# The norm's input transposed by the host: scaling x^T in place, with only the inverse roots turned on TensorE

## The chip, the cores and the metric

The kernel runs on one core of a Trainium2 chip. The metric is the device time of one execution in microseconds. The core has TensorE (PE in the profile, its weight loads PEld), VectorE (DVE), ScalarE (ACT), GpSimd (POOL) and SyncE (SP), which here does nothing but start DMA transfers, all in one queue. Each engine takes its own instructions strictly in the order in which the program holds them, and waits on semaphores for what other engines and transfers deliver.

## The reference

One block of a streaming encoder over 2048 tokens of width 1024, in float32. What matters here is its beginning:

```
xn = rms_norm(h, norm_gain[layer])          # x * rsqrt(mean(x*x) + eps) * gain
proj = xn @ w_in[layer]
qa, ka, va, ga, qb, kb, vb, gb, iq, ik, iw, za, zb = jnp.split(proj, offsets, axis=-1)
```

Two kinds of attention follow, one over neighbouring chunks, one over the 256 keys per query that an indexer (`iq`, `ik`, `iw`) picks; then gates, an output product and a second norm. A product on TensorE contracts over the partitions of both operands, so `xn` is needed with the 1024 features on partitions (8 slices of 128) and the tokens along the free axis: as x^T.

## The kernel before

Tokens are taken in 16 tiles of 128, in the order `order = [8..15, 0..7]`. A first stage goes over the tiles once: it norms a tile, keeps it transposed and split into a rounded high part `xh` and the rest `xl` (three products of such parts replace one in full precision), and projects it on 424 columns (`wih`, `wil`) for the indexer and the shared key and value of the second attention. `xh` and `xl` have two slots of 512 tokens each; for the first eight tiles both are also written to DRAM (`xsD`) and read back much later. Then the main stage multiplies `xh`, `xl` with all other columns of the weights (`acc` in the rows), while the indexer's logits and the search for the top keys run beside it; attention and output follow.

The functions of the first stage, in the order of the code: `load_x` starts a tile's transfer two tiles ahead; `norm` squares the tile on ScalarE with a sum (`sq`, `ss`), takes ten small VectorE steps to the inverse root (`rsqrt`, L141 to L147), scales the tile in place by root and gain (L248), turns it on TensorE in 8 pieces of 128x128 (L253, into PSUM tiles `tr` and `trl`), and splits it (L256 on ScalarE, L257 on VectorE, both from PSUM). `project` has 24 matmuls of 424 columns (L274), then a copy `tok` on ScalarE (L278) and 13 small GpSimd steps for the rotary angles (`rope`, and L281). `keys` splits key and indexer key (`kk`), turns three pieces (L304) and stores them. `prep` fetches and splits the weights of the main stage (L172 to L176: a copy that gates the transfer, ScalarE's rounding, GpSimd's subtraction). The loop calls `norm(i + 1)`, `project(i)`, `keys(i - 1)`.

The code's order isn't the program's: a scheduler takes what is ready by its own estimate and fixes the order of each engine before the run, so matmuls of the main stage can stand among those of the last projections, and the pieces of `norm` for one tile among steps of others. Buffers come from pools; a tile with the same tag waits until the one before it is free.

## Time and profile before

| what | value |
|---|---|
| time, median of 3 runs | 2105.91 us (2104.52 to 2106.01) |
| time of the profiled execution | 2103.23 us |
| its span | 2101.3 us |
| TensorE busy | 2033.5 us, 97% |
| VectorE, ScalarE, GpSimd busy | 65%, 58%, 42% |
| granted TensorE clock, mean | 0.997 |

The median lies 2.7 us above the profiled execution, whose time has 1.9 us outside its span. "Busy" counts overlapping instructions once. The page's 40 slices are 52.5 us each; the first stage is the first two and a bit.

### The profile page before, as it was taken

To read this page: it belongs to the slowest core of one execution; us is meant where nothing else is said; L and a number is where in the kernel's file an instruction comes from. 1 tells how busy PE (TensorE), PEld (TensorE's weight loads), DVE (VectorE), ACT (ScalarE), POOL (GpSimd) and SP (SyncE) were. 2 spreads that over 40 slices of the span, in tenths; PEclk is the share of its full clock that TensorE was granted. 3 is DMA by queue.
4 is the path that set the end of the run, shared out by engine and by line. 5 is a ranking of instruction groups with operands and counts; after the bars stand their busy time and mean duration, and the time that the engine had idled before them with its cause. 6 is when DMAs were issued, how large, how long until landed. Compare 5 with 4: busy or idle time off the path is not lost.

```text
span 2101.3 us, 34534 instructions
## 1 busy us (share of the span) xinstructions
PE 2033.5 (97%) x11138; PEld 1745.2 (83%) x11138; DVE 1367.2 (65%) x3719; ACT 1224.7 (58%) x2440; POOL 887.7 (42%) x1081
## 2 busy tenths in 40 slices
PE   7999999998999999999999999999999999999998
PEld 7888778778888878888897888888888888887786
DVE  7824796959888596601334777866886688875444
ACT  5544555555565665412444878966896688873221
POOL 5653445454433443312232555446444543443420
PEclk9999999999999999999999999999999999999999
DMA  8642234353455323323757865567345732145642
GB/s 275 191 145 92 101 125 139 114 179 108 152 198 216 125 76 129 113 101 119 244 185 211 254 197 177 163 193 227 112 132 184 225 123 68 56 135 182 209 152 90
DMA packets 228282, 326.57 MB, mean 155 GB/s; under 512 B 19584, under 2 KB 113152, under 8 KB 227456
## 3 DMA queue, kind: packets, MB, share of 16 engines
q1 hardware_dynamic: 228096, 324.32, 47.2%
q8 instruction: 88, 1.44, 0.3%
q14 instruction: 98, 0.80, 0.1%
HBM read 211.03 MB, written 113.21 MB: 154 GB/s over the span
## 4 chain that ended last, share of the span: by engine, by line
PE 42%; DMA 4%; ACT 2%; issue 1%; DVE 1%; POOL 1%; SPq 0%; DVEq 0%; ACTq 0%; POOLq 0%
PE d L570 7%; PE po L1135 6%; PE s L874 6%; PE O L899 6%; PE pt L891 5%; PE acc L570 4%; PE O L809 3%; PE pt L799 3%; PE s L764 2%; DMA mf<-mD 1%; DMA dst<-wB 1%; DVE P L695 1%; POOL dw L937 0%; ACT P L769 0%; DMA qB<-eht 0%
## 5 line engine op out<-in xcount | busy, mean ns | idle before, releaser
L570 PE MATMUL acc<-xh,wt 128*128 128x512 f32 x2304 | 732.5, 392 | 0.0
L570 PEld LDWEIGHTS acc<-xh,wt 128*128 128x128 f32 x2304 | 431.8, 188 | 88.9
L570 PE MATMUL acc<-xl,wt 128*128 128x512 f32 x1152 | 451.1, 392 | 0.0
L176 POOL TENSOR_TENSOR wt<-wst,wt 128x512 fp32r<-128x512 f32 x156 | 209.4, 1355 | 289.5 <-ACT wt L175 268.0
L716 POOL TENSOR_TENSOR ptl<-pf,pth 128x512 fp32r<-128x512 f32 (+1 forms) x144 | 179.6, 1248 | 216.7 <-ACT pf L712 163.3
L570 PEld LDWEIGHTS acc<-xl,wt 128*128 128x128 f32 x1152 | 216.9, 188 | 44.2
L392 ACT ACTIVATE r<-lg 128x512 f32<-128x512 f32 (+2 forms) x304 | 157.1, 540 | 162.4 <-DVE sc L400 49.9
L719 DVE TENSOR_TENSOR ptl<-pt,pth 128x512 fp32r<-128x512 f32 (+1 forms) x288 | 188.1, 660 | 53.6 <-ACT pth L718 52.7
L400 DVE SCALAR_TENSOR_TENSOR sc<-r,iw,sc 128x512 f32<-128x512 f32 (+2 forms) x190 | 137.0, 726 | 112.6 <-POOL sc L398 71.0
L874 PE MATMUL s<-kBt,qsB 128*128 128x512 f32 (+3 forms) x640 | 187.5, 384 | 4.7 <-DMA kBt<-kB 2.3
L718 ACT ACTIVATE pth<-pt 128x512 fp32r<-128x512 f32 (+1 forms) x288 | 161.4, 578 | 26.1 <-PE pt L891 11.7
L891 PE MATMUL pt<-ident,P 128*128 128x128 f32 x1088 | 166.5, 273 | 1.1 <-DVE ptl L719 0.5
L877 ACT ACTIVATE P<-P,mx 128x128 f32<-128x128 f32 (+15 forms) x128 | 154.6, 1209 | 15.6 <-DVE mx L695 15.0
L397 POOL TENSOR_SCALAR r<-r,iw 128x512 f32<-128x512 f32 (+2 forms) x76 | 57.1, 752 | 224.2 <-ACT r L392 187.6
L899 PE MATMUL O<-pth,vBt 128*128 128x256 f32 x544 | 148.1, 290 | 1.9 <-DVE yb L909 1.4
L434 ACT ACTIVATE jk<-sc,st 128x640 int8<-128x640 f32 (+6 forms) x63 | 91.6, 1454 | 99.9 <-DVE st L454 98.7
L899 PE MATMUL O<-ptl,vBt 128*128 128x256 f32 x544 | 147.7, 297 | 1.0 <-POOL ptl L716 0.6
L695 DVE CUSTOM_DVE_ANT_0 P<-s,mk,mx 128x512 f32<-128x512 f32 (+2 forms) x192 | 125.1, 652 | 33.9 <-PE s L874 28.2
L175 ACT ACTIVATE wt<-wst 128x512 fp32r<-128x512 f32 x156 | 93.9, 627 | 78.9 <-DMA wst<-wP 75.5
L891 PEld LDWEIGHTS pt<-ident,P 128*128 128x128 f32 x1088 | 128.1, 141 | 9.5 <-ACT pf L712 1.5
L390 PE MATMUL lg<-ikT,iqT 128*128 128x512 f32 (+2 forms) x304 | 106.6, 382 | 22.6 <-ACT r L392 16.7
L937 POOL TENSOR_TENSOR dw<-dst,dw 128x512 fp32r<-128x512 f32 x64 | 83.0, 1296 | 99.3 <-ACT dw L936 82.4
(222 smaller groups left out, 4461.6 us busy)
## 6 DMA issues: line engine op xcount, KB each, us to landing
wst<-wP SPq DMA_DIRECT2D x156, 256.0 KB, 2.9
qs<-qA SPq DMA_DIRECT2D x128, 128.0 KB, 3.2
kk<-kA SPq DMA_DIRECT2D x56, 256.0 KB, 4.2
vs<-vA SPq DMA_DIRECT2D x56, 256.0 KB, 3.3
bias<-biasD SPq DMA_DIRECT2D x32, 320.0 KB, 4.7
xt<-x SPq DMA_DIRECT2D x16, 512.0 KB, 4.5
sBD<-ef SPq DMA_DIRECT2D x32, 256.0 KB, 2.0
sAD<-ef SPq DMA_DIRECT2D x32, 256.0 KB, 2.0
```

The source lines that it names most:

```text
L176: nc.gpsimd.tensor_tensor(wt[:, 1, k:k + 4, c * 128:(c + 1) * 128], st, f32(hi), op=OP.subtract)
L392: nc.scalar.activation(r[:, :w], lg[:, :w], AF.Relu)
L400: nc.vector.scalar_tensor_tensor(o_, r[:, :w], wv, o_, op0=OP.mult, op1=OP.add)
L570: nc.tensor.matmul(acc, a, b, start=(i == 0), stop=(i == n - 1))
L695: nc.vector.tensor_tensor_reduce(dst, ps_, add, 1.0, FMAX if first else mx, OP.add, OP.min, accum_out=mx)
L716: nc.gpsimd.tensor_tensor(lo, pf, f32(hi), op=OP.subtract)
L718: nc.scalar.activation(hi, src, AF.Copy)
L719: nc.vector.tensor_tensor(lo, src, f32(hi), op=OP.subtract)
L874: nc.tensor.matmul(s_ps[:, :w], q[:, h, :], kBt[:, m, a:a + w], start=(m == 0), stop=(m == 1))
L877: nc.scalar.activation(P[:, e, :n], P[:, e, :n], AF.Exp, bias=mx[:, e:e + 1], scale=-1.0, accum_out=st["sum"][:, (u % 2) * 2 + e:(u % 2) * ...
L891: nc.tensor.transpose(pt[:, k, e, :], P[:, e, (kt + k) * 128:(kt + k + 1) * 128], ident)
L899: nc.tensor.matmul(o_, vBt[:, kt + k, :], src[:, k, :], start=(kt + k == 0 and n_ == 0), stop=(kt + k == b and n_ == 1), skip_group_check= ...
```

## The change

The host also writes x transposed, as 16 tiles of 128 features x 8 slices x 128 tokens (`xT`), and the gain as 128 x 8. `load_x` fetches both forms of a tile. `norm` squares the plain form as before; the root, one number per token, is widened by ScalarE to a 128x128 tile `rb` (the same number along a row), and TensorE turns that one piece, so that PSUM holds the roots along the free axis on every partition. GpSimd multiplies x^T by the gain, VectorE multiplies the result by the turned roots, in place, and the split now reads SBUF and takes the whole tile at once (the first tile in two halves, as before).

```diff
         def load_x(i):
-            xts[i] = xp.tile([128, D], F32, name="xt", tag="xt", bufs=XTB)
-            nc.sync.dma_start(xts[i], x[order[i] * 128:(order[i] + 1) * 128, :])
+            xts[i] = (xp.tile([128, D], F32, name="xt", tag="xt"),
+                      xp.tile([128, KT, 128], F32, name="xT", tag="xT", bufs=XTB))
+            nc.sync.dma_start(xts[i][0], x[order[i] * 128:(order[i] + 1) * 128, :])
+            nc.sync.dma_start(xts[i][1], io["xT"][order[i]])
...
-        gain = wp.tile([128, D], F32, name="gain")
-        nc.sync.dma_start(gain, bass.AP(tensor=io["g1"].tensor, offset=io["g1"].offset, ap=[[0, 128], [1, D]]))
+        gain = wp.tile([128, KT], F32, name="gain")
+        nc.sync.dma_start(gain, io["g1"])
...
-            xt = xts.pop(i)
+            xt, xT = xts.pop(i)
...
             r = rsqrt(xp, ss, "rs")
-            xn = xt
-            w_ = D // HALVES if i < 1 else D
-            for a in range(0, D, w_):
-                nc.vector.scalar_tensor_tensor(xn[:, a:a + w_], xt[:, a:a + w_], r, gain[:, a:a + w_], op0=OP.mult, op1=OP.mult)
+            rb = xp.tile([128, 128], F32, name="rb0", tag="rb0")
+            nc.scalar.activation(rb, r.to_broadcast([128, 128]), AF.Copy)
+            nc.gpsimd.tensor_tensor(xT, xT, gain[:, :, None].to_broadcast([128, KT, 128]), op=OP.mult)
+            tr = next_tr()
+            nc.tensor.transpose(tr[:, 0, :], rb, ident)
             g, o = divmod(t, 4)
-            for hf in range(2):
-                tr = next_tr()
-                for k in range(4):
-                    nc.tensor.transpose(tr[:, k, :], xn[:, (hf * 4 + k) * 128:(hf * 4 + k + 1) * 128], ident)
-                sl = (slice(None), slice(hf * 4, hf * 4 + 4), slice(o * 128, o * 128 + 128))
+            w_ = KT // HALVES if i < 1 else KT
+            for a in range(0, KT, w_):
+                sl = (slice(None), slice(a, a + w_), slice(o * 128, o * 128 + 128))
+                xn = xT[:, a:a + w_]
+                nc.vector.tensor_tensor(xn, xn, tr[:, 0:1, :].to_broadcast([128, w_, 128]), op=OP.mult)
                 xh_, xl_ = xh[SLOT[g]][sl], xl[SLOT[g]][sl]
-                nc.scalar.activation(xh_, tr, AF.Copy)
-                nc.vector.tensor_tensor(xl_, tr, f32(xh_), op=OP.subtract)
+                nc.scalar.activation(xh_, xn, AF.Copy)
+                nc.vector.tensor_tensor(xl_, xn, f32(xh_), op=OP.subtract)
...
+    d["xT"] = np.ascontiguousarray(d["x"].reshape(NT, 128, KT, 128).transpose(0, 3, 2, 1))
+    d["g1"] = np.ascontiguousarray(a["norm_gain"][0].reshape(KT, 128).T)
```

What the scheduler makes of it, at three places (`x2` is twice in a row). First VectorE at the start of the program, before: the inverse roots of the first two tiles are interleaved, and the scaling of the first tile (L248, two halves) stands in the middle of the second tile's root.

```order
L146 SCALAR_TENSOR_TENSOR rsa<-rsy,ss 128x1
L248 SCALAR_TENSOR_TENSOR xt<-xt,rsy,gain 128x512 x2
L147 SCALAR_TENSOR_TENSOR rsy<-rsa,rsy 128x1
L146 SCALAR_TENSOR_TENSOR rsa<-rsy,ss 128x1
L215 TENSOR_TENSOR wil<-wis,wih 128x424
L147 SCALAR_TENSOR_TENSOR rsy<-rsa,rsy 128x1
```

The same place after the change; L257 is now the product with the turned roots, L260 the subtraction that gives `xl`.

```order
L146 SCALAR_TENSOR_TENSOR rsa<-rsy,ss 128x1
L147 SCALAR_TENSOR_TENSOR rsy<-rsa,rsy 128x1
L257 TENSOR_TENSOR xT<-xT,tr 128x512 x2
L217 TENSOR_TENSOR wil<-wis,wih 128x424 x2
L257 TENSOR_TENSOR xT<-xT,trl 128x1024
L260 TENSOR_TENSOR xl_122<-xT,xh_120 128x4x128 x2
L217 TENSOR_TENSOR wil<-wis,wih 128x424 x2
L260 TENSOR_TENSOR xl_122<-xT,xh_120 128x8x128
```

The whole of the second tile's root now stands ahead of the first tile's product, and the first `xl` behind two pieces of `wil` and the second tile's product.

Second, ScalarE at the start, before: squares of two tiles, four pieces of the weights' high part `wih`, then the two halves of the first `xh`.

```order
L242 ACTIVATE sq,ss<-xt 128x1024 x2
L214 ACTIVATE wih<-wis 128x424 x4
L256 ACTIVATE xh_120<-tr 128x4x128
L256 ACTIVATE xh_120<-trl 128x4x128
L214 ACTIVATE wih<-wis 128x424 x4
```

After the change, `rb_213` and `rb_245` being the widened roots of the first and second tile:

```order
L244 ACTIVATE sq,ss<-xt 128x1024 x2
L248 ACTIVATE rb_213<-rsy 128x128
L216 ACTIVATE wih<-wis 128x424 x2
L248 ACTIVATE rb_245<-rsy 128x128
L216 ACTIVATE wih<-wis 128x424 x2
L259 ACTIVATE xh_120<-xT 128x4x128 x2
L216 ACTIVATE wih<-wis 128x424 x4
L259 ACTIVATE xh_120<-xT 128x8x128
```

The second tile's root now stands ahead of the third piece of `wih` and of the first `xh`.

Third, TensorE behind the projection of the twelfth tile, where the first matmuls of the main stage (L570) stand; `pi_1378` is the thirteenth tile's accumulator. Before:

```order
L274 MATMUL pi<-wih,xl_122 128x424
L570 MATMUL acc<-xh_120,wt 128x512
L570 MATMUL acc<-xl_122,wt 128x512
L274 MATMUL pi_1378<-wih,xh_121 128x424
L274 MATMUL pi_1378<-wil,xh_121 128x424
L570 MATMUL acc<-xh_120,wt 128x512 x2
```

The same place after the change, where the main stage's matmuls are L573, the projection is L277 and the thirteenth tile's accumulator `pi_1314`; L251 turns the widened roots, L307 pieces of a key tile.

```order
L277 MATMUL pi<-wih,xl_122 128x424
L573 MATMUL acc<-xh_120,wt 128x512
L573 MATMUL acc<-xl_122,wt 128x512
L251 MATMUL trl<-ident,rb_1410 128x128
L307 MATMUL tr<-ident,kk 128x128 x3
L573 MATMUL acc<-xh_120,wt 128x512 x2
L573 MATMUL acc<-xl_122,wt 128x512
```

In the order after the change the thirteenth projection begins behind all the twelve that stand there, in the one before behind the first two. In all, 24 of the main stage's matmuls now stand ahead of the last projection's last matmul, where 11 stood before. On GpSimd the order begins with the gain products of the first two tiles, the four `wil` pieces that it had, and the gain product of the third tile, in a row, where it had the four `wil` pieces alone; the other thirteen gain products stand among the steps of `rope`. From some 500 TensorE instructions on (out of 11,000) the orders of the two programs are the same on every engine.

## Rows read from the trace of the kernel before

**Rows 1.** The page: busy time of the engines over the span.

```profile
PE 2033.5 (97%) x11138; PEld 1745.2 (83%) x11138; DVE 1367.2 (65%) x3719; ACT 1224.7 (58%) x2440; POOL 887.7 (42%) x1081
```

**Rows 2.** Busy time by stretch of the first stage. Columns: stretch and its length in us; for each engine us busy and (x instructions), in the order PE, PEld, DVE, ACT, POOL; then the granted clock, the DMA engines' mean busy share, and GB/s.

```profile
0.00:20.00 20.00, 7.08 (x25) 6.00 (x26) 12.74 (x37) 11.25 (x20) 9.44 (x91) 1.00 0.81 277
20.00:40.00 20.00, 19.78 (x112) 18.78 (x111) 13.98 (x54) 9.67 (x25) 8.00 (x27) 1.00 0.83 242
40.00:60.00 20.00, 20.00 (x121) 18.85 (x119) 15.38 (x58) 11.61 (x30) 13.18 (x52) 1.00 1.04 309
...
20.00:60.00 40.00, 39.78 (x231) 37.63 (x229) 29.36 (x109) 21.28 (x54) 21.18 (x78) 1.00 0.94 275
60.00:100.00 40.00, 36.71 (x212) 33.64 (x211) 33.40 (x110) 22.93 (x57) 25.43 (x84) 1.00 0.60 188
```

**Rows 3.** Groups of instructions in the first 145 us, by line, engine and operation: busy us and mean ns of one, then idle time of the engine before them.

```profile
L248 DVE SCALAR_TENSOR_TENSOR xt<-xt,rsy,gain 128x1024 f32<-128x1024 f32 (+1 forms) x17 | 22.8, 1343 | 1.0 <-DMA gain<-g 0.6
L257 DVE TENSOR_TENSOR xl<-tr,xh 128x512 fp32r<-128x512 f32 x17 | 11.6, 683 | 4.2 <-ACT xh L256 4.2
L253 PE MATMUL tr<-ident,xt 128*128 128x128 f32 x68 | 11.4, 292 | 9.8 <-DVE xt L248 9.5 <-DVE xl L257 0.2
L253 PE MATMUL trl<-ident,xt 128*128 128x128 f32 x60 | 10.5, 296 | 4.5 <-DVE xt L248 2.5 <-DVE ikT L307 1.6 <-DVE xl L257 0.3
...
L176 POOL TENSOR_TENSOR wt<-wst,wt 128x512 fp32r<-128x512 f32 x13 | 16.7, 1289 | 17.3 <-ACT wt L175 17.1
L398 POOL TENSOR_TENSOR sc<-sc,r 128x384 f32<-128x384 f32 x1 | 1.0, 1022 | 0.1
```

**Rows 4.** TensorE in order of time: start us, us, instruction, xcount. Neighbours overlap; the step from one start to the next is what an instruction takes of the engine.

```profile
103.83 0.36 PE L274 MATMUL pi<-wih,xh 128*128 128x424 f32 x1
104.02 0.36 PE L274 MATMUL pi<-wil,xh 128*128 128x424 f32 x1
...
107.31 1.04 PE L253 MATMUL tr<-ident,xt 128*128 128x128 f32 x8
108.10 0.44 PE L274 MATMUL pi<-wih,xh 128*128 128x424 f32 x1
...
119.50 0.62 PE L570 MATMUL acc<-xh,wt 128*128 128x512 f32 x2
...
120.19 0.62 PE L570 MATMUL acc<-xh,wt 128*128 128x512 f32 x2
```

**Rows 5.** VectorE and GpSimd in order of time, at four moments: start us, us, engine, instruction.

```profile
13.34 3.49 POOL L215 TENSOR_TENSOR wil<-wis,wih 128x424 fp32r<-128x424 f32 x2 [0.47 <-ACT wih L214]
15.80 0.68 DVE L257 TENSOR_TENSOR xl<-tr,xh 128x512 fp32r<-128x512 f32 x1
...
25.06 0.22 DVE L146 SCALAR_TENSOR_TENSOR rsa<-rsy,ss 128x1 f32<-128x1 f32 x1
25.51 1.35 DVE L248 SCALAR_TENSOR_TENSOR xt<-xt,rsy,gain 128x1024 f32<-128x1024 f32 x1
25.74 1.18 POOL L230 TENSOR_TENSOR rpk<-tok,cosK 128x8 f32<-128x8 f32 x1
...
83.97 1.33 DVE L146 SCALAR_TENSOR_TENSOR rsa<-rsy,ss 128x1 f32<-128x1 f32 x1
83.99 1.29 POOL L176 TENSOR_TENSOR wt<-wst,wt 128x512 fp32r<-128x512 f32 x1
...
91.23 2.54 POOL L176 TENSOR_TENSOR wt<-wst,wt 128x512 fp32r<-128x512 f32 x2
91.36 1.17 DVE L147 SCALAR_TENSOR_TENSOR rsy<-rsa,rsy 128x1 f32<-128x1 f32 x1
92.57 2.29 DVE L248 SCALAR_TENSOR_TENSOR xt<-xt,rsy,gain 128x1024 f32<-128x1024 f32 x1
```

**Rows 6.** The start of the program, and the copies that end the first and the last tile's projection (L278), in order of time: start us, us, engine, instruction, and in brackets the engine's idle time before it and what ended it.

```profile
4.75 1.06 ACT L242 ACTIVATE sq<-xt 128x1024 bf16<-128x1024 f32 x1 [2.73 <-DMA xt<-x]
6.02 1.06 ACT L242 ACTIVATE sq<-xt 128x1024 bf16<-128x1024 f32 x1
8.69 1.42 DVE L248 SCALAR_TENSOR_TENSOR xt<-xt,rsy,gain 128x512 f32<-128x512 f32 x2 [0.63 <-DMA gain<-g]
9.74 2.11 ACT L214 ACTIVATE wih<-wis 128x424 fp32r<-128x424 f32 x4 [2.58 <-DMA wis<-wI]
12.38 0.72 PE L274 MATMUL pi<-wih,xh 128*128 128x424 f32 x1 [0.90 <-ACT xh L256]
17.55 0.70 PE L274 MATMUL pi<-wih,xl 128*128 128x424 f32 x1
20.88 0.56 PE L274 MATMUL pi<-wih,xl 128*128 128x424 f32 x1
21.23 0.56 PE L274 MATMUL pi<-wih,xh 128*128 128x424 f32 x1
...
24.00 0.52 ACT L278 ACTIVATE tok<-pi 128x424 f32<-128x424 f32 x1 [3.75 <-PE pi L274]
...
117.97 0.52 ACT L278 ACTIVATE tok<-pi 128x424 f32<-128x424 f32 x1 [0.22 <-PE pi L274]
```

**Rows 7.** DMA issues of the first 150 us by transfer: engine, kind, xcount, KB each, median us from issue to landing.

```profile
xt<-x SPq DMA_DIRECT2D x16, 512.0 KB, 4.5
xsD<-xh SPq DMA_DIRECT2D x8, 512.0 KB, 5.6
```

More of the change, by code (lines that the diff above doesn't have):

```diff
@@ L1186, in layouts @@
     d["x"] = np.ascontiguousarray(a["x"][0])
-    d["g1"] = np.ascontiguousarray(a["norm_gain"][0])
+    d["xT"] = np.ascontiguousarray(d["x"].reshape(NT, 128, KT, 128).transpose(0, 3, 2, 1))
+    d["g1"] = np.ascontiguousarray(a["norm_gain"][0].reshape(KT, 128).T)
     d["g2"] = np.ascontiguousarray(a["final_norm_gain"])
```

## The prediction

> **What bounds the kernel now.** I read the busy line of the page first: TensorE works 97% of the span and no other engine comes near it [rows 1], so what the change takes off TensorE should come off the time, wherever TensorE is also the limit in the stretch that is touched. That stretch is the first stage alone, which lasts until the copy at 117.97 us [rows 6]; behind it the order on every engine is that of before. So the question is by how much the end of this stage moves. From the first tile's copy at 24.00 to the last one's, fifteen tiles take 93.97 us, 6.26 us a tile [rows 6].
>
> The windows come next [rows 2]. From 20 to 60 us TensorE is busy 39.78 of 40 us: it is the limit there. From 60 to 100 us it is busy 36.71 of 40, so something else already stops it for 3.3 us. VectorE is the second busiest: 29.36 and 33.40 us in the two windows, 62.76 of 80 us, which is 78%, or 4.91 us of each 6.26 us tile, with 1.35 us free. The groups say who stops TensorE: ahead of the transposes it idles 9.8 + 4.5 us, of which 9.5 + 2.5 us end with VectorE's scaling L248 [rows 3] (the start's waits are in it). VectorE's chain for a tile is thus almost as long as TensorE's work.
>
> The last view, VectorE and GpSimd side by side in order of time, shows how they disturb each other [rows 5]. A 128x1 step L146 takes 0.22 us at 25.06, but 1.33 us at 83.97, where GpSimd's 1.29 us subtraction L176 begins 0.02 us later; both end together. L147 (1.17 us) and L248 (2.29 instead of 1.35 us) are stretched in the same way at 91.36 and 92.57, under two such subtractions. It goes both ways: GpSimd's 128x8 product at 25.74 takes 1.18 us and ends with VectorE's L248. But L257 at 15.80, whose first source is in PSUM, takes its usual 0.68 us in the middle of 3.49 us of GpSimd work. So what is stretched are VectorE's steps with both sources in SBUF.
>
> **The change part by part.** *TensorE.* Eight transposes a tile become one. Eight take 0.79 us from start to start (107.31 to 108.10), 0.099 us each [rows 4]; 112 fewer are 11.1 us, 0.69 us a tile.
>
> *VectorE.* L248 (1.34 us) and two L257 (0.68 us each) go, 2.70 us a tile [rows 3]. The product of x^T with the turned roots reads PSUM as L257 did: twice 0.68 = 1.37 us. The new `xl` reads two SBUF sources of 1024 as L248 did: 1.34 us. Together 2.71 us; I take no change. But the last step of a tile, which TensorE waits for, can now be stretched by GpSimd, where L257 could not.
>
> *GpSimd.* Sixteen products of 128x1024 with the gain are new. The trace has none of that size there: 512 columns take 1.29 us and 384 take 1.02 [rows 3], 0.27 us per 128 more, so by estimate 1.29 + 4 x 0.27 = 2.4 us. Bounds: 1.29 us, if a broadcast operand made it as cheap as half the size, and 2.54 us, two subtractions one after the other at 91.23 [rows 5]. GpSimd itself has room: 21.18 and 25.43 us of 40 [rows 2], 3.3 to 4.0 us a tile, so 5.7 to 6.4 with the product. What counts is what the product costs VectorE. Beside it VectorE can do what reads PSUM, the 1.37 us product. Bounds for the loss are nothing (the product falls wholly into VectorE's idle 1.35 us and its PSUM work) and 2.54 us. I take 1.7 us, 2.4 less half of the 1.37: the order gives VectorE ten root steps in a row for the next tile, and a gain product is ready as soon as x^T has landed, with nothing that keeps it out of their way. A tile then costs VectorE 4.91 + 1.7 = 6.6 us, more than TensorE's 6.26 - 0.69 = 5.57 and more than the old 6.26. VectorE becomes the limit: 15 x 0.35 = +5.2 us.
>
> From 91.23 to 94.86 us VectorE did just two steps, which alone take some 0.2 and 1.34 us, beside and behind 2.54 us of GpSimd [rows 5]: 2.1 us lost of 2.5. So the loss can be larger than I take; with 2.54 in full a tile is 7.45 us, 15 x 1.19 = +17.9 us in place of +5.2. I stay at 1.7 because those were steps of one kind in a row and a tile has 1.37 us of the other.
>
> *ScalarE.* One `rb` of 128x128 more, and `xh` in one piece instead of two. It costs between nothing and a 128x1024 square's 1.06 us [rows 6]; ScalarE is busy 22.93 of 40 us [rows 2], so this is hidden and I take nothing. If the cover went, it would be that 1.06 us a tile.
>
> *Transfers.* x^T adds 16 x 512 KB; a tile of x lands 4.5 us after its issue [rows 7]. The gain shrinks by 512 KB. Up to 60 us the engines of the DMA were idle for 20 x (0.19 + 0.17) = 7.2 us [rows 2]. The x^T of ten tiles, 5.2 MB at some 300 GB/s, is 17.5 us; less the idle 7.2 and the gain's 1.7 the tenth tile is 8.6 us later. It was fetched two tiles ahead, 12.5 us, of which 4.5 were the landing: 8 us of cover, so I take nothing.
>
> *The start.* Before, the squares of the first two tiles began at 4.75 and 6.02, the gain ended L248's wait at 8.69, and the first matmul began at 12.38, waiting for `xh` [rows 6]. Now x^T of two tiles, 1 MB, comes ahead of the gain in the one queue; I put the gain at 9 us, and the gain products of two tiles at 9.0 to 13.8. The second tile's six root steps with two SBUF sources lie under them and now stand ahead of the first tile's work on VectorE, and its `rb` stands ahead of `xh` on ScalarE (the order rows). I take `xh` 5 us later and `xl`, which let TensorE go on at 17.55, 3 us later, at 20.5; TensorE catches none of this up: +4 us for the first tile's end. Bounds: nothing, if the roots slip through ahead, and three gain products in a row, +7.1 us.
>
> *Main stage's matmuls.* 24 instead of 11 stand before the last projection's end. They fill TensorE's waits if VectorE is the limit: 13 x 0.23 us (three from 119.50 to 120.19 [rows 4]) = -3.0 us.
>
> **Sum.** +5.2 + 4.0 - 3.0 = +6.2 us on the profiled 2103.2 is 2109.4; the median lies 2.7 us above the profile, so 2112 us.
>
> **Rivals.**
>
> 1. *VectorE's loss is smaller, a draw.* With 1.2 us lost a tile takes 6.1 us: 15 x -0.16 = -2.4, +4.0 - 3.0 = -1.4 us, 2104.5. For it: half of the product lies beside PSUM work. Against: the six root steps of a tile, each of which can meet GpSimd.
>
> 2. *TensorE's saving comes through.* VectorE's idle 1.35 us takes all of the loss, TensorE stays the limit: -11.1 + 4.0 = -7.1 us, 2099. For it: 39.78 of 40 us busy. Against: the idle of 3.3 us from 60 to 100 us that is already there.
>
> 3. *Transfers limit the first ten tiles.* From 40 to 60 us the DMA engines were full already (1.04 [rows 2]). If x^T of the tenth tile is 2 us too late, the other six gain 6 x 0.69: +2 - 4.1 - 3.0 = -5 us, 2101. Against it: the 8 us of cover.
>
> 4. *Slower: the two engines work in single file.* GpSimd's 3.3 us a tile and VectorE's 4.6 - 1.37 = 3.2 us without L257 (20 to 60 us) make 6.5 us, of which some 1.0 is a wait counted twice (1.18 us instead of some 0.2 at 25.74 [rows 5]). If all of it excludes each other, 5.5 + 2.4 = 7.9 us a tile: 15 x 1.64 = +24.6, +4.0 - 3.0 = +25.6 us, 2131. It decides as soon as GpSimd has no idle left at a tile's end. Against it: much of a short step is overhead, in which nothing may be held.
>
> The Trainium skill ("SBUF — State Buffer", section "Who interferes with whom") speaks for this rival: a VectorE instruction with two SBUF inputs contends with a GpSimd instruction that reads SBUF, and of the shared pair of ports it says that whoever issues first holds it for the whole instruction while the other fully blocks. By that rule the trace agrees where one such meeting can be seen (1.33 us against 0.22), and the sum would be the rival's 2131; whether short steps block in full too, it doesn't show.
>
> **How the numbers follow.** Forecast 0.42 (its own range 2108 to 2118, from +4 to +7.1 at the start and 1.6 to 2.0 us lost), rival one 0.20, two 0.15, three 0.10, four 0.13. The range 2098 to 2126 leaves out the better part of the second rival's lower half and most of the fourth. A measurement tells 0.2%, 4.2 us, from no change: faster means below 2101.7, slower above 2110.1. Faster: most of 0.15, 0.06 of the third, 0.03 of the first, 0.24. Slower: 0.36 of the forecast, 0.13, 0.02 of the first, 0.51. The rest, 0.25, is no change.
>
> **What would show it.** Right: L249 on GpSimd at about 2.4 us; root steps (L146, L147) and `xl` (L260) with means well above 0.2 and 1.34 us; VectorE busy above 90% from 30 to 110 us, TensorE waiting there for `xl`; the first copy near 28 us and the last near 124. Wrong: TensorE gapless with a tile at 5.6 us (rival two); gaps that end with the landing of x^T, the DMA share at 1 (three); GpSimd gapless and 7.9 us a tile (four). If the gain product took about 1.3 us, the forecast's main term would be gone; if the first copy stayed at 24 us, the start's.

## The result: 1.0% slower, and the profile after

The changed kernel takes 2126.87 us (median of four runs, 2126.11 to 2128.12) against 2105.96 us before: 20.9 us slower, a ratio of 1.0098 with a 95% interval of 1.0082 to 1.0114. The forecast was 2112 us and a range up to 2126. The side was right; the size was more than three times what was expected. The profiled execution took 2126.88 us with a span of 2125.1, 23.8 us more than before, and this is what can be taken apart.

The page's busy line, which answers to [rows 1]:

```profile
PE 2030.7 (96%) x11026; PEld 1738.5 (82%) x11026; DVE 1386.0 (65%) x3704; ACT 1228.9 (58%) x2441; POOL 916.1 (43%) x1097
```

TensorE has 112 instructions less, 11.1 us of work by the prediction's price, yet its busy time fell by 2.8 us only. The windows show where; they answer to [rows 2], with the same columns. The last two are the stretch from the first `tok` copy to the last, before and after:

```profile
20.00:60.00 40.00, 35.83 (x165) 32.88 (x166) 35.33 (x93) 20.63 (x45) 29.26 (x72) 0.91 0.97 317
60.00:100.00 40.00, 28.82 (x136) 26.39 (x136) 32.82 (x97) 21.27 (x50) 25.70 (x62) 0.87 0.77 250
...
24.00:117.97 93.97, 90.35 (x523) 84.31 (x522) 67.44 (x221) 53.22 (x133) 57.73 (x203) 1.00 0.68 207
...
27.82:135.68 107.86, 92.15 (x447) 84.05 (x446) 79.97 (x216) 57.15 (x136) 82.70 (x222) 0.91 0.77 251
```

From 20 to 100 us TensorE is busy 64.65 us where it was busy 76.49, and the granted clock, 1.00 throughout before, is 0.91 and 0.87. VectorE works 68.15 of 80 us (62.76 before), GpSimd 54.96 (46.61). Between the two copies TensorE is idle for 15.7 us, 3.6 before. The tiles show it as well: the copies that end the first and the last projection, in order of time with their start and duration in us, answer to [rows 6].

```profile
27.82 0.51 ACT L281 ACTIVATE tok<-pi 128x424 f32<-128x424 f32 x1
...
135.68 0.52 ACT L281 ACTIVATE tok<-pi 128x424 f32<-128x424 f32 x1
```

The first tile ends 3.8 us later, and a tile now takes (135.68 - 27.82) / 15 = 7.19 us instead of 6.26. In the groups of the first 145 us (busy us and mean ns; then idle time before and what ended it), which answer to [rows 3], TensorE's waits are, behind the first 20 us, nearly all those ahead of L277. The line of before is shown first:

```profile
L297 DVE TENSOR_TENSOR kk<-tok,kk 128x64 fp32r<-128x64 f32 x16 | 3.6, 223 | 4.7 <-ACT kk L295 4.7
```

```profile
L277 PE MATMUL pi<-wih,xh 128*128 128x424 f32 x128 | 50.7, 397 | 11.4 <-ACT tok L281 7.5 <-ACT xh L259 3.9
L277 PE MATMUL pi<-wih,xl 128*128 128x424 f32 x128 | 49.8, 390 | 5.3 <-DVE xl L260 4.8 <-DVE ss L245 0.5
L249 POOL TENSOR_TENSOR xT<-xT,gain 128x1024 f32<-128x1024 f32 x16 | 32.8, 2058 | 8.1 <-DMA gain<-g 6.2 <-DMA xT<-xT 1.6
L260 DVE TENSOR_TENSOR xl<-xT,xh 128x1024 fp32r<-128x1024 f32 (+1 forms) x17 | 23.3, 1372 | 3.9 <-ACT xh L259 3.9
L146 DVE SCALAR_TENSOR_TENSOR rsa<-rsy,ss 128x1 f32<-128x1 f32 x48 | 16.9, 358 | 0.9
L300 DVE TENSOR_TENSOR kk<-tok,kk 128x64 fp32r<-128x64 f32 x16 | 15.5, 966 | 2.2 <-ACT kk L298 2.1
```

The gain product L249 takes 2.06 us on average. Short VectorE steps pay for it, one above all: L300, a 128x64 subtraction, averages 0.97 us, where the same subtraction (L297) took 0.22 before.

One stall, the longest, shows the mechanism. These are rows of the four engines in order of time, start and duration in us, from 74 to 86 us (shorter steps, two squares of ScalarE and TensorE's matmuls up to 79.2 us are left out):

```profile
74.66 3.80 POOL L249 TENSOR_TENSOR xT<-xT,gain 128x1024 f32<-128x1024 f32 x2
75.11 1.59 DVE L299 TENSOR_TENSOR kk<-tok,kk 128x128 fp32r<-128x128 f32 x1 [2.00 <-ACT kk L297]
76.62 1.92 DVE L300 TENSOR_TENSOR kk<-tok,kk 128x64 fp32r<-128x64 f32 x1
78.46 1.21 DVE L257 TENSOR_TENSOR xT<-xT,tr 128x1024 f32<-128x1024 f32 x1
79.21 0.27 PE L251 MATMUL trl<-ident,rb 128*128 128x128 f32 x1
79.70 1.06 ACT L259 ACTIVATE xh<-xT 128x1024 fp32r<-128x1024 f32 x1 [4.48 <-DVE xT L257]
80.07 1.90 POOL L249 TENSOR_TENSOR xT<-xT,gain 128x1024 f32<-128x1024 f32 x1 [1.61 <-DMA xT<-xT]
80.79 2.26 DVE L260 TENSOR_TENSOR xl<-xT,xh 128x1024 fp32r<-128x1024 f32 x1 [1.12 <-ACT xh L259]
82.97 1.21 DVE L257 TENSOR_TENSOR xT<-xT,trl 128x1024 f32<-128x1024 f32 x1
84.21 1.06 ACT L259 ACTIVATE xh<-xT 128x1024 fp32r<-128x1024 f32 x1 [1.23 <-DVE xT L257]
85.18 0.51 ACT L281 ACTIVATE tok<-pi 128x424 f32<-128x424 f32 x1
85.73 0.72 PE L277 MATMUL pi<-wih,xh 128*128 128x424 f32 x1 [6.25 <-ACT tok L281]
```

Two gain products in a row hold two short `kk` subtractions, which end when the products end (76.6 and 78.5 us). Only then can VectorE scale the next x^T, only then can ScalarE round it, and a third product stretches `xl` to 2.26 us. The copy `tok` stands behind the second `xh` in ScalarE's order, and TensorE needs the accumulator that this copy frees: it idles 6.25 us, though nothing between 79.2 and 85.7 us takes long by itself. Two things meet here, the products and ScalarE's order; without the products (e1 below) one wait for a `tok` copy remains, of 4.1 us.

The idle time costs a second time. After it the steps from one matmul to the next are 0.35 us, later in the same tile 0.20, as they are throughout [rows 4] (0.19):

```profile
86.25 0.56 PE L277 MATMUL pi<-wil,xh 128*128 128x424 f32 x1
86.61 0.56 PE L277 MATMUL pi<-wih,xl 128*128 128x424 f32 x1
...
89.28 0.35 PE L277 MATMUL pi<-wil,xh 128*128 128x424 f32 x1
89.47 0.36 PE L277 MATMUL pi<-wih,xl 128*128 128x424 f32 x1
```

That is the lower of the clock's two levels, 1.2 instead of 2.4 GHz, granted after TensorE stood idle; the view of the windows shows a granted clock of 0.50 from 84 to 89 us. Nine steps at some 0.16 us more are 1.4 us here. (At the start TensorE goes in steps of 0.35 us too, until 21.6 us before and 24.2 us after, though the windows show 1.00 there; the granted clock of these first 25 us can't be read off them.)

The rest of the loss lies where no order was changed. The chain of waits of both kernels has two long pieces of TensorE work in the tail, the same ones (start us, us, what), first before, then after:

```profile
1110.76 21.81 PE acc L570 x96
...
1995.27 97.93 PE po L1135 x432
```

```profile
1124.76 21.81 PE acc L573 x96
...
2019.06 97.93 PE po L1138 x432
```

The first is 14.0 us late, the second 23.8. So 14 us are lost up to the first point, nearly all in the first stage, and 9.8 us between the two, by a program that reads the same on every engine there.

### The profile page after: what moved, and what is told of

The parts are those of the page before. It is cut to its first block, busy times and chain, and to the rows that moved or that the text cites. A ratio compares the mean times of both kernels' runs of the same rounds, so it can differ in the third digit from the quotient of the medians.

```text
span 2125.1 us, 34350 instructions
## 1 busy us (share of the span) xinstructions
PE 2030.7 (96%) x11026; PEld 1738.5 (82%) x11026; DVE 1386.0 (65%) x3704; ACT 1228.9 (58%) x2441; POOL 916.1 (43%) x1097
## 4 chain that ended last, share of the span: by engine, by line
PE 40%; DMA 5%; ACT 2%; DVE 2%; issue 2%; POOL 1%; SPq 0%; DVEq 0%; ACTq 0%; POOLq 0%
PE d L573 7%; PE po L1138 6%; PE O L902 5%; PE s L877 5%; PE pt L894 5%; PE acc L573 4%; PE O L812 3%; PE pt L802 2%; PE s L767 2%; DMA dst<-wB 1%; DMA mf<-mD 1%; DMA dst<-wA 1%; DVE P L698 1%; DMA ost<-wO 0%; POOL dw L940 0%
## 5 line engine op out<-in xcount | busy, mean ns | idle before, releaser
L573 PE MATMUL acc<-xh,wt 128*128 128x512 f32 x2304 | 731.6, 392 | 0.0
L573 PEld LDWEIGHTS acc<-xh,wt 128*128 128x128 f32 x2304 | 431.1, 188 | 88.9
L573 PE MATMUL acc<-xl,wt 128*128 128x512 f32 x1152 | 450.1, 391 | 0.0
L573 PEld LDWEIGHTS acc<-xl,wt 128*128 128x128 f32 x1152 | 216.4, 188 | 43.8
L880 ACT ACTIVATE P<-P,mx 128x128 f32<-128x128 f32 (+15 forms) x128 | 154.5, 1208 | 17.5 <-DVE mx L698 16.8
L393 PE MATMUL lg<-ikT,iqT 128*128 128x512 f32 (+2 forms) x304 | 106.7, 382 | 23.5 <-ACT r L395 17.4
```

The source lines that it names most:

```text
L573: nc.tensor.matmul(acc, a, b, start=(i == 0), stop=(i == n - 1))
L880: nc.scalar.activation(P[:, e, :n], P[:, e, :n], AF.Exp, bias=mx[:, e:e + 1], scale=-1.0, accum_out=st["sum"][:, (u % 2) * 2 + e:(u % 2) * ...
```

## The experiments

Two quantities are read from every profile. The *stage's end* is the last `tok` copy less 0.23 us for each main-stage product ahead of it (counted in the trace: 12 before, 30 after), so that fillers don't count as delay: 115.2 us before, 128.8 after, +13.6. In brackets it is taken apart into the *start* (the first `tok` copy) and the *tiles* (from the first copy to the last, less 0.23 us for each filler). The *tail* is the distance between the two chain pieces above: 884.5 us before, 894.3 after. They come from one execution each; the times are medians over more runs, and the runs of the kernel before beside them had 2108.5 to 2109.0 us (2105.96 beside the first comparison). A *filler* is such a main-stage product.

| run | median us | ratio to before, 95% interval | stage's end against before (start, tiles) | tail us |
|---|---|---|---|---|
| changed, first comparison | 2126.87 | 1.0082 to 1.0114 | +13.6 (+3.8, +9.8) | 894.3 |
| e1 no gain product | 2121.13 | 1.0041 to 1.0073 | +3.4 (-1.9, +5.3) | 886.9 |
| e2 gain on VectorE | 2129.14 | 1.0073 to 1.0106 | +5.1 (-3.4, +8.5) | 897.9 |
| e3 product alone | 2130.28 | 1.0082 to 1.0120 | +20.0 (+3.7, +16.4) | 893.2 |
| e4 loads alone | 2127.17 | 1.0065 to 1.0109 | +12.6 (-0.6, +13.2) | 889.4 |
| e5 x^T declared | 2109.82 | 0.9996 to 1.0019 | -0.9 (-0.4, -0.5) | 887.2 |
| e6 halves | 2133.39 | 1.0081 to 1.0127 | +12.1 (+4.4, +7.7) | 895.3 |
| e7 no gain, no loads | stage only | | -2.6 (-1.9, -0.6) | |
| e9 gain in pieces | 2154.06 | 1.0197 to 1.0231 | +34.9 (+5.0, +29.9) | 894.4 |
| e10 changed, again | 2131.06 | 1.0085 to 1.0120 | +14.3 (+3.8, +10.4) | 893.3 |
| e11 changed, padded | 2124.55 | 1.0061 to 1.0085 | +14.5 (+3.6, +11.0) | 887.9 |
| e12 before, whole piece | 2110.19 | 0.9999 to 1.0022 | -0.1 (+0.1, -0.2) | 887.5 |
| e14 before, half | 2108.69 | 0.9991 to 1.0010 | +0.4 (-1.5, +1.9) | 885.7 |
| e15 before, quarter | 2112.64 | 1.0001 to 1.0026 | +0.7 (-0.6, +1.3) | 894.8 |
| e16 before, three quarters | 2111.54 | 1.0004 to 1.0023 | -0.7 (-1.3, +0.7) | 890.5 |

(e5 is the program of before once more, and the padded kernels e12 to e16 leave its orders alone. What they show against before, up to 0.9 us at the stage's end and up to 2 us for start and tiles, is the scatter of one profile against another.) Between the stage's end and the tail the changed kernel loses 0.4 us, and 2.0 in e10; e5 shows 2.8. e1 to e4, e6 and e9 have other orders of the main stage and lose 4.5 to 10.5 us there, which was not followed.

**e1: the changed kernel without the gain product.**

```diff
-            nc.gpsimd.tensor_tensor(xT, xT, gain[:, :, None].to_broadcast([128, KT, 128]), op=OP.mult)
```

> The changed kernel without GpSimd's gain product, so the first norm's gain is left out; x^T, its transfers, the widened roots and the one transpose stay. Theory A (the gain products hold VectorE's steps with two SBUF sources, and TensorE waits behind these): the first stage loses its 14 us of waits, the last tok copy comes at 112 to 120 us instead of 135.7, and the time is 2098 to 2108 us. Theory B (the 8.4 MB of x^T or the new order of ScalarE, with the tok copies behind the next tile's xh, makes the waits): the last copy stays at 130 us or later, the time at 2118 or more.

The copy came at 126.66 us, between the two theories; with 35 main-stage products ahead of it instead of 12 the stage's end is +3.4 us, so 10.2 of the 13.6 us go with the product. The larger part of that is the start: the first copy comes at 22.06 us, 5.8 earlier than in the changed kernel; in the fifteen tiles the product makes 4.4 us. The time fell to 2121 only, theory B's range. The scheduler made another order of the main stage as well: between the stage's end and the tail this kernel loses 8.9 us that the changed one doesn't. The norm's values are others here, but VectorE, ScalarE and TensorE execute as many instructions as in the changed kernel. Theory A holds for most of the stage's delay; for B's transfers speak its windows, where the DMA share is 1.05 and TensorE still waits:

```profile
20.00:60.00 40.00, 35.83 (x176) 32.31 (x174) 28.37 (x101) 21.45 (x49) 19.82 (x78) 0.91 1.05 330
60.00:100.00 40.00, 32.66 (x157) 30.09 (x158) 28.99 (x104) 25.28 (x56) 18.11 (x68) 0.91 0.86 280
```

VectorE's `kk` subtraction (L299 in this kernel) is back at 0.30 us:

```profile
L299 DVE TENSOR_TENSOR kk<-tok,kk 128x64 fp32r<-128x64 f32 x16 | 4.8, 301 | 12.0 <-ACT kk L297 12.0
```

**e2: the gain taken by VectorE.**

```diff
-            nc.gpsimd.tensor_tensor(xT, xT, gain[:, :, None].to_broadcast([128, KT, 128]), op=OP.mult)
...
-                nc.vector.tensor_tensor(xn, xn, tr[:, 0:1, :].to_broadcast([128, w_, 128]), op=OP.mult)
+                for k in range(w_):
+                    nc.vector.scalar_tensor_tensor(xn[:, k], xn[:, k], gain[:, a + k:a + k + 1], tr[:, 0, :], op0=OP.mult, op1=OP.mult)
```

> The changed kernel with the gain taken by VectorE: eight SCALAR_TENSOR_TENSOR of 128x128 (x^T times gain times turned root, one source in PSUM) replace GpSimd's product and VectorE's one product. Theory A: GpSimd's lock is gone, VectorE pays about 0.8 us a tile more (8 x 0.25 for 1.2); its 4.9 us a tile become 5.7 of 6.26, so the last copy comes at 114 to 122 us and the time is 2100 to 2110 us. Theory B: no gain on the changed kernel, 2120 or more.

The stage's end came back from +13.6 to +5.1, of which 7.2 us are the start and only 1.3 the tiles: there the product costs 3.2 us on VectorE (e2 against e1), 4.4 on GpSimd. A piece took 0.34 us where 0.25 was expected:

```profile
L257 DVE SCALAR_TENSOR_TENSOR xT<-xT,gain,trl 128x128 f32<-128x128 f32 x64 | 17.5, 340 | 1.8 <-PE trl L250 1.7
```

In time this was a miss: 2129 us. What the stage won was lost behind it, 10.5 us up to the tail's beginning under another order, and 13 us in the tail.

**e3: the product alone, in the kernel before.**

```diff
             r = rsqrt(xp, ss, "rs")
+            jk = xp.tile([128, D], F32, name="jk", tag="jk", bufs=1)
+            nc.gpsimd.tensor_tensor(jk, xt, gain, op=OP.mult)
```

> The kernel before, plus one GpSimd product of 128x1024 a tile (x times gain, into a tile that nobody reads); nothing else of the change. Theory A: these products alone cost most of the first stage's loss: the last copy comes 8 us or more later than 117.97, the time is 2114 us or more. Theory B: it moves by less than 4 us, 2102 to 2110.

+20.0 us at the stage's end, 2130 us: sixteen GpSimd instructions whose result nobody reads cost as much as the whole change. (The scaling overwrites the tile that they read and so has to come behind them; in the trace each of them ends at least 0.8 us before its tile's scaling begins, and no wait is put down to one.) With two full SBUF sources one takes 2.50 us:

```profile
L246 POOL TENSOR_TENSOR jk<-xt,gain 128x1024 f32<-128x1024 f32 x16 | 39.9, 2495 | 12.0 <-DMA xt<-x 7.8 <-DMA gain<-g 4.0
```

**e5: x^T declared, not read.**

```diff
+    d["xT"] = np.ascontiguousarray(d["x"].reshape(NT, 128, KT, 128).transpose(0, 3, 2, 1))
```

> The kernel before with the 8.4 MB tensor x^T among its inputs, and no instruction that reads it. The changed kernel loses 10 us more between 1040 us and its end, where the two orders are the same. If that is the place of the buffers in DRAM, this kernel loses them too (2112 us or more, all of it behind 1000 us); if it is the state that the first stage leaves behind, the time is that of before, 2104 to 2108.

No change (1.0008). Declaring the input isn't what makes the tail longer. It is also a second look at the program of before: its tail is 887.2 us here, 884.5 in the first profile, so some 3 us of a tail are scatter.

**e6: every tile in halves.**

```diff
-            w_ = KT // HALVES if i < 1 else KT
+            w_ = KT // HALVES
```

> The changed kernel with every tile in two halves (product with the roots, xh and xl of 512 columns each), as the first tile has it. Theory D: from the turned root to the first matmul VectorE's 1.2 us product and ScalarE's 1.0 us xh of the whole tile stand one behind the other, and TensorE waits for them because the root's transpose stands at the end of the tile before; in halves some 1.1 us a tile come back, 10 to 17 us in all, 2110 to 2117 us on the scale of the first comparison (before at 2106). Theory A (lock by the gain product): the halves change less than 4 us.

No gain: 2133 us, the stage's end some 2 us earlier than in e10 and 1.4 than in the first profile. Theory D's 10 to 17 us didn't come; the serial steps from the root to the first matmul are not the main thing that TensorE waits for.

**e7: e1 with x^T loaded for three tiles only.**

```diff
-            nc.gpsimd.tensor_tensor(xT, xT, gain[:, :, None].to_broadcast([128, KT, 128]), op=OP.mult)
...
-                      xp.tile([128, KT, 128], F32, name="xT", tag="xT", bufs=XTB))
+                      xp.tile([128, KT, 128], F32, name="xT", tag="xT", bufs=XTB) if i < XTB else xts[i - XTB, 1])
+            xts[i, 1] = xts[i][1]
...
-            nc.sync.dma_start(xts[i][1], io["xT"][order[i]])
+            if i < XTB:
+                nc.sync.dma_start(xts[i][1], io["xT"][order[i]])
```

> The kernel of e1 (no gain product), and of x^T only the first three tiles are loaded; later tiles scale these again, so the values are not the input's. Theory C (the transfers of x^T are what holds e1, where the DMA engines' share was 1.05 from 20 to 60 us): 8 us or more faster than e1, about 2098 to 2106 where before is 2106. Theory D (the serial chain from the turned root to the first matmul holds it): within 4 us of e1, some 12 us slower than before.

Its total of 3205 us answers nothing: from 800 to 1600 us TensorE is busy for 204 of 800 us, while VectorE goes on with the search for the top keys; it executes 5818 instructions in all instead of 3704, with values that are not the input's. The first stage does answer: it ends at -2.6 us, 6.0 us before e1's, all of it in the tiles. So the loads cost 6.0 us there, where theory C expected 8 or more, by one profile each. With neither product nor loads the fewer transposes bring 2.6 us of the 11.1; what keeps the rest wasn't followed (TensorE is still idle for 10.6 us between the first and the last copy).

**e4: the loads alone, in the kernel before.**

```diff
             nc.sync.dma_start(xts[i], x[order[i] * 128:(order[i] + 1) * 128, :])
+            xTs[i] = xp.tile([128, KT, 128], F32, name="xT", tag="xT", bufs=1)
+            nc.sync.dma_start(xTs[i], io["xT"][order[i]])
...
             r = rsqrt(xp, ss, "rs")
+            jk = xp.tile([128, 8], F32, name="jk", tag="jk", bufs=1)
+            nc.scalar.activation(jk, xTs[i][:, 0, 0:8], AF.Copy)
```

> The kernel before with the transfers of x^T added (one slot, read by one ScalarE copy of 8 columns a tile, not used). Theory C: 6 us or more slower than before, with the stage ending later than 124 us. If the transfers are hidden: within 3 us of before.

The copy came at 133.29 us and the time at 2127: the transfers are not hidden here. The share was 0.94 and 0.60 in these two windows before [rows 2]:

```profile
20.00:60.00 40.00, 38.52 (x225) 35.59 (x223) 31.05 (x110) 23.32 (x59) 18.37 (x83) 1.00 0.99 304
60.00:100.00 40.00, 33.68 (x177) 29.88 (x178) 25.83 (x95) 22.33 (x57) 17.97 (x68) 0.96 0.94 293
```

Part of the 12.6 us may be this kernel's own: its one slot makes ScalarE wait for x^T in its order (16.8 us between 18 and 125 us, in the view of the waits), which the changed kernel's three slots don't.

```profile
ACT jk L248 <- DMA xT<-xT: 16.8, 10, 2.7
```

So the price of the loads in the changed kernel rests on e7 against e1.

**e9: the gain product in eight pieces.**

```diff
-            nc.gpsimd.tensor_tensor(xT, xT, gain[:, :, None].to_broadcast([128, KT, 128]), op=OP.mult)
+            for k in range(KT):
+                nc.gpsimd.tensor_scalar(xT[:, k], xT[:, k], gain[:, k:k + 1], None, op0=OP.mult)
```

> The changed kernel with the gain product cut into eight TENSOR_SCALAR of 128x128 a tile on GpSimd, one per slice with its gain per partition: about the same work, each piece short. If the length of one product is what hurts (VectorE's step waits until the whole instruction ends), VectorE's kk subtraction L300 falls from 0.97 us to 0.5 or less and the time by 5 us or more. If GpSimd's total time counts, no change within 4 us, or slower by the pieces' own overhead.

Far worse, 2154 us: a piece takes 0.66 us, so a tile's product grows from 2.06 to 5.3 us, and GpSimd is busy 39.4 of the 40 us from 20 to 60.

```profile
L250 POOL TENSOR_SCALAR xT<-xT,gain 128x128 f32<-128x128 f32 x125 | 80.3, 658 | 9.2 <-DMA gain<-g 6.2 <-DVE kk L300 2.2
```

The question of the length of one piece is answered by half. VectorE's `kk` subtraction fell to 0.32 us, as was expected if it is held for one GpSimd instruction at a time:

```profile
L301 DVE TENSOR_TENSOR kk<-tok,kk 128x64 fp32r<-128x64 f32 x15 | 4.8, 318 | 2.3 <-ACT kk L299 2.3
```

What short pieces would be worth in time it doesn't say, since the total grew too and GpSimd itself had hardly any idle time left.

**e10: the changed kernel again**, the same file, for comparison with e11.

> The changed kernel itself once more, beside the next three on the same chip: it is what e11 is compared with. Expected as before: some 20 us above the kernel before, a first stage that ends 13 us later and 8 to 12 us more lost behind 1000 us.

+22.3 us in time; in the profile +14.3 at the stage's end and +8.8 in the tail: the first profile repeats.

**The tail, one event.** The distance between the two profiles, 14.0 us where the tail begins, grows at several places. The largest step was followed: at 1640 us of before it is 18.86 us, at 1680 it is 21.97. These are SP's issues of the load for `dw` and of `ta`, before and after (start us, us):

```profile
1639.44 0.46 SPq L934 DMA_DIRECT2D dst<-wB  x1
...
1640.45 0.42 SPq L949 DMA_DIRECT2D ta<-tD  x1
```

```profile
1658.30 0.46 SPq L937 DMA_DIRECT2D dst<-wB  x1
...
1659.31 1.84 SPq L952 DMA_DIRECT2D ta<-tD  x1
```

The last one takes 1.84 us instead of 0.42 (in e10 it takes 0.42, and the loss comes all the same). ScalarE's `dw`, which waits for `dst`, starts 1.53 us later than it would at the same distance (1664.07 instead of 1643.68 + 18.86 = 1662.54). The view of the DMA queues from 1659.0 to 1661.3 us of the changed kernel has one packet in it that the same stretch of before (1640.2 to 1642.5) has not:

```profile
q8 instruction: 1, 0.02, 4.5%
...
mD<-dt SPq DMA_DIRECT2D x1, 256.0 KB, 5.7
ta<-tD SPq DMA_DIRECT2D x1, 256.0 KB, 6.0
```

```profile
mD<-dt SPq DMA_DIRECT2D x1, 256.0 KB, 4.2
ta<-tD SPq DMA_DIRECT2D x1, 256.0 KB, 4.4
```

It is a fetch of instructions: 0.02 MB, 4.5% of 16 engines over 2.3 us, 1.7 us of one engine, and the transfers that meet it land 1.5 us later. TensorE stands idle for 2.47 us while it waits for `dw`, and then its granted clock falls to half:

```profile
1666.00:1669.40 3.40, 3.40 (x12) 2.91 (x11) 1.85 (x4) 2.78 (x7) 3.40 (x4) 0.51 0.62 177
```

So the step of 3.1 us is 1.5 us of landing and, by difference, some 1.6 of clock. The nine profiles of the two programs, padded or not, bear it out. In three of them (the changed kernel, e10, and e15 below) a fetch begins 0.9 to 1.6 us behind the issue of the load for `dw`: `ta` lands after 5.9 to 6.0 us, the granted clock falls to half there, and the distance from before grows by 3.0 to 3.1 us. In before, e5, e11, e12 and e16 no fetch begins within 5 us of that issue, and in e14 one begins 0.2 us behind it: `ta` lands after 4.1 to 4.8 us, and the distance changes by less than 0.5 us.

The span has 88 such packets of 16 KB, and TensorE 11138 matmuls and as many weight loads: a piece is some 256 instructions, so they look like TensorE's code, and in the padded kernels below, where TensorE alone has more instructions, they move. The change takes 224 instructions out ahead of the tail, and every later fetch meets another transfer. That was theory E.

**e11: the changed kernel with its instruction count filled up.**

```diff
+        dum = ps.tile([128, 4, 128], F32, name="dum", tag="tr1")
+        for j in range(112):
+            nc.tensor.matmul(dum[0:16, j % 4, 0:16], ident[:, 0:16], ident[:, 0:16], start=True, stop=True)
         norm(0)
```

> The changed kernel with 112 matmuls of 16x16 on the identity at the start of TensorE's program, where TensorE has nothing to do; they bring the number of its instructions back to that of the kernel before, and every engine's order stays word for word. Theory E: TensorE's code is fetched in pieces of 16 KB by the same DMA engines that carry the data, and a fetch makes the transfer that it meets some 1.2 us later; the change takes 224 instructions out ahead of the tail, so that each fetch falls on another transfer there than before. Then the tail comes back to that of before: 6 to 12 us faster than the changed kernel, all of it behind 1000 us, while the first stage stays 13 us late. Theory F (the tail is slow for another reason, a state that the first stage leaves): within 3 us of the changed kernel.

6.5 us faster than e10 in time (the intervals 1.0061 to 1.0085 and 1.0085 to 1.0120 just touch), with the stage as late as e10's (+14.5) and the tail 5.4 us shorter. Instructions that compute nothing made the kernel faster. They shift the fetches by another amount than was meant (see e12).

**e12, e14 to e16: the kernel before, shifted.** The same lines in the kernel before, with 64, 32, 16 and 48 matmuls.

> The kernel before with 64 such matmuls at the start of TensorE's program: 128 instructions, half a piece of code; the order of everything else stays. Theory E: the fetches fall on other transfers in the tail, the time moves by 4 us or more, likelier up (to 2112 to 2120) than down. Theory F: within 2 us of before.

In the trace each of these matmuls is two:

```profile
1.51 3.60 PE L312 MATMUL dum<-ident 128*16 128x16 f32 x128 [1.51 <-POOL ident masks.py:199]
```

So 64 of them, with their weight loads, are 256 instructions, a whole piece and not a half. That makes it the control: three successive fetches of the tail begin 517.0, 497.5 and 478.7 us ahead of the end before and 516.5, 497.0 and 477.9 here, and the tail (887.5 us) is that of e5 (887.2). (e13, which was to shift by a whole piece, gave no result.) e11's 112 are 448 instructions, 224 more than were taken out; this comes within 32 instructions of a whole piece, so the fetches fell close to the old places by luck.

> The kernel before with 32 matmuls of 16x16 at the start of TensorE's program, each of which the program issues as two loads and two products (64 of e12's appear as 128): 128 instructions, a true half of a 16 KB piece; e12's were a whole piece and moved no fetch. Theory E: the fetches fall half a piece elsewhere in the tail, and the time is 2113 us or more where before is 2108.7, all of the loss behind 1000 us. Theory F: within 2 us of before.

> The same with 16 matmuls, 64 instructions, a quarter of a piece. Theory E: another time again, between 2108 and 2120 us, and not that of before by necessity; the changed kernel's place, 224 instructions earlier, is near a quarter of a piece less than a whole. Theory F: within 2 us of before.

> The same with 48 matmuls, 192 instructions, three quarters of a piece. Theory E: some time between 2108 and 2120 us that differs from the other two; if a place is better than that of before, the time falls below 2107. Theory F: within 2 us of before.

A half piece changes nothing (2108.69 us), three quarters and a quarter cost 0.04% to 0.23% and 0.01% to 0.26%. The quarter puts the fetches where the changed kernel has them: two successive ones begin 1074.7 and 1060.2 us ahead of the end in its profile and 1074.2 and 1059.3 in the changed kernel's. Its tail is 894.8 us, like the changed kernel's 894.3 and 893.3, with a first stage that ends within 0.7 us of that of before, and its order:

```profile
1111.55 21.81 PE acc L573 x96
...
2006.30 97.93 PE po L1138 x432
```

Theory E holds in its direction: the same place of the fetches, the same tail, whatever came ahead. Its size is not settled, but for the 3.0 to 3.1 us of the step above: in profiled executions the place costs 7 to 10 us (894.8 against 884.5 to 887.5), in the timed medians 3.7 us for e15 and 6.5 us between e10 and e11. Its prediction for the half was wrong: not every shift costs, it depends on which transfers are met. And the other variants (e1 to e9) have tails between 887 and 898 us whose parts weren't separated.

None of the runs beats the kernel before.

## Why the prediction was too low, point by point

- **What bounds the stage, and the side.** The side was right, and the reason in part: the saving of TensorE did not come through, and the gain product on GpSimd makes most of the stage's delay. Without it the stage's end moves back by 10.2 us (e1), and alone it costs 20.0 (e3). But VectorE did not become the limit, and three terms that the sum left out push to the same side (the transfers, the clock, the tail); that the side came out is partly luck.
- **Who stops TensorE: a row misread.** The 9.5 and 2.5 us of waits for VectorE's scaling in [rows 3] are one wait each and both lie in the first 20 us; behind them, up to the last copy, TensorE waits 3.5 us in the trace of before, and none of it for L248. So the rows did not show that VectorE's chain was the next limit.
- **The start: +4.0 us.** Right, by the steps named: the gain landed at 10.27 (9 was taken), the first matmul came at 17.52 (17.4), the first with `xl` at 21.25 (20.5), the first copy at 27.82 (28). The second tile's root steps lie under the gain products as foreseen:

```profile
10.27 3.75 POOL L249 TENSOR_TENSOR xT<-xT,gain 128x1024 f32<-128x1024 f32 x2 [6.23 <-DMA gain<-g]
10.49 1.70 DVE L146 SCALAR_TENSOR_TENSOR rsa<-rsy,ss 128x1 f32<-128x1 f32 x1
12.22 1.82 DVE L147 SCALAR_TENSOR_TENSOR rsy<-rsa,rsy 128x1 f32<-128x1 f32 x1
```

- **The product's length, 2.4 us, and VectorE's steps.** Close: 2.06, and 1.9 undisturbed. The product with the roots took 1.21 us where 1.37 was taken, `xl` 1.37 where 1.34 was.
- **6.6 us a tile, +5.2 us: this step failed.** It took the stage as one engine's sum, VectorE's busy time plus what it loses, and let everything else flow around it. Measured: 7.19 us a tile, 13.9 us in fifteen tiles, so the term was 8.7 us too small. VectorE's part was, if anything, taken too large: it was busy 79.97 us between the first and the last copy, 5.33 us a tile, 85% of the time from 20 to 100 us and not the 90% that were to show the forecast right. The steps that it listed were hardly stretched, but for L146 (0.36 us; 0.26 before): L147 0.19, `xl` 1.37 (1.16 in e1). The one that was stretched most, `kk`, it did not list. TensorE's longest wait was for a `tok` copy on ScalarE, behind an `xh`, behind a VectorE step, behind two GpSimd products: a loss on one engine was passed on through three orders, and each link added its own wait.
- **What the fifteen tiles lost in its place.** For TensorE the 13.9 us are, by estimate from the rows above: 12.1 us more idle time, some 7.5 us of lower clock, 4.1 us for 18 more fillers, less 10.4 us for 105 transposes, 13.3 in all. By cause, fillers taken off (+9.8): -0.6 with neither product nor loads (e7), +6.0 with the loads (e1), +4.4 with the product. The order of taking away matters: added alone to the kernel before, the product costs 16.4 in the tiles (e3) and the loads 13.2 (e4, part of it its own).
- **The clock: left out.** In four stretches of the stage (34.5 to 41.3, 68.6 to 72.0, 82.3 to 89.1 and 119.8 to 123.2 us) the granted clock is 0.50, each time after TensorE stood idle; it is busy 16.4 us in them, and at 0.19 instead of 0.35 us a step that is the 7.5 us. Before, there is no such stretch between the first and the last copy. TensorE's waits could not be priced as mere waits.
- **The transfers, taken at nothing: this failed too.** 6.0 us between e7 and e1. The sum compared lateness with two tiles of cover; in the changed kernel as in e1 the share is near 1 from 20 to 60 us, and a tile of x lands 6.0 us after its issue instead of 4.5 [rows 7]. By which waits the 6.0 us come is not shown: in the changed kernel a single wait of 1.6 us ends with the landing of x^T. Rival three had this mechanism, but forecast a faster kernel by it.
- **The main stage's matmuls: -3.0 us.** Right in kind. 18 more (30 instead of 12) stood ahead of the last copy, some 4 us. (They stand ahead of that copy, so by the sum's own terms it would have come near 127 us and not near 124.)
- **The orders are the same behind the first stage, so only the stage's end counts: this step failed too.** The premise was right and the conclusion wrong. 9.8 us of the span's 23.8 arise behind 1110 us. The place of TensorE's code fetches makes part of it: 3.1 us by the step at 1640 us, between 3.7 and 10 us by e11 and e15. The rest stays open.

The sum as it came: +3.8 at the start, +13.9 for fifteen tiles, -4.1 for the fillers, +0.4 up to the tail, +9.8 in the tail, 23.8 us. (The forecast's own range, 2108 to 2118, leaves out the 2.7 us between profile and median that the sum has; with them it is 2111 to 2120, still below what was measured.) The fourth rival, engines in single file at 7.9 us a tile, was nearer in size, but it decides "as soon as GpSimd has no idle left": GpSimd had 25 of 80 us idle. A short step is held for a whole product, all the same: 0.97 us on average for a subtraction that takes 0.30 in e1, steps that end with the products at 76.6 and 78.5 us, and 0.32 us where the product comes in short pieces (e9). The Trainium skill's rule ("SBUF — State Buffer", "Who interferes with whom") that the shared pair of ports is an exclusive lock agrees with these rows.

## What to carry to other kernels

Before giving GpSimd a long SBUF product, look up which short VectorE steps with two SBUF sources stand in its time, and follow the in-order queue of each engine behind them to the one that waits at the end: the price is the length of that chain, not the product's share of a busy time. A transfer into a stretch whose DMA share is already near 1 should not be taken at nothing. And a comparison of two programs that differ in the number of TensorE's instructions can carry several microseconds of chance in whatever follows, as it did here; shifting the old program by parts of a piece, as e12 to e16 do, shows how much.

## What was not expected of the hardware

- Instruction fetches disturb data: a 16 KB piece on the DMA engines, 88 of them in 2101 us, made the transfers that it met land 1.5 us later, in three profiles of nine at the same place; with the fall of the clock behind it that was 3.0 to 3.1 us. In the profiles of before and its padded forms the same tail took 885 to 895 us, of which some 3 us are scatter.
- On GpSimd, 128x128 TENSOR_SCALAR with a scalar per partition takes 0.66 us in the company of VectorE, eight of them 5.3 us, against 2.06 us for one TENSOR_TENSOR of 128x1024 with a broadcast operand; with two full operands that product takes 2.50 us.
- A 16x16 float32 matmul appears as two in the trace (64 in the program of e12, 128 in its trace).
